# One fixed-order stream of 1 MB weight halves in the expert stage of a hybrid diffusion backbone

## The chip, the cores and the metric

One Trainium2 chip; the program runs on one of its cores. The metric is device microseconds of one execution. A page of the profile calls the engines PE (TensorE, with PEld for its weight loads), DVE (VectorE), ACT (ScalarE), POOL (GpSimd) and SP (the queue that issues most DMAs).

## What is computed

A trunk layer over 1024 tokens of width 1024: modulated RMSNorm, a token mixer, then an expert-choice MoE, and a last RMSNorm. Four fifths of the time goes to the MoE, in fp32:

```python
cap = EC_CAPACITY * n // N_EXPERTS          # 128 tokens for each of 16 experts
aff = softmax(h @ w_router)
g, idx = lax.top_k(swapaxes(aff, 1, 2), cap)
xg = h[bidx, idx]
hid = silu(xg @ w_gate) * (xg @ w_up)       # (128, 1024) @ (1024, 2816), twice
y = (hid @ w_down) * g[..., None]           # (128, 2816) @ (2816, 1024)
out = zeros_like(h).at[bidx, idx].add(y)
```

## The kernel before

After a prologue (the mixer, the router, and the token lists of experts 0 and 1), `moe` walks over 16 experts `e` and six column blocks `j` of each: five of 512 columns, one of 256. `gate_up(e, j)` multiplies the gathered tokens with a block of w_gate and of w_up, `down` of the block before multiplies its hidden block with rows of w_down into `y`.

A product in fp32 is made of three products of rounded parts (`mm3`, L607): ScalarE rounds a weight tile (`hi`, L226), VectorE subtracts (`lo`, L227), and TensorE multiplies x_hi by hi, x_hi by lo and x_lo by hi, in this order (L610). `xgh`/`xgl` are the parts of the tokens, `hh`/`hl` those of the hidden block. The weights are the moving operand.

Weights are loaded as 2 MB units into five raw slots `raw` (`load_unit`, L1535, DMA at L1541) and split in halves of 2048 columns into four `hi`/`lo` pairs (`hl_tile`, L1524), used in rotation: three pairs lie in the left pool `ma`, one in the right pool `mo`, where `xgh`, `xgl`, `hh` and `hl` lie too. A half is 12 matmuls of 512 columns (24 of 256 in the last block). Pair n is written again once TensorE has read it: with four pairs, the split of half m+4 waits for TensorE's last matmul of half m.

Beside the weights there are small steps:
- after each `gate_up`: `hid` (Silu on ScalarE at L1565, product on VectorE at L1566), four transposes `ht` on TensorE (L1570), `hh`, `hl`.
- once per expert `prep` (L1441): VectorE makes a one-hot tile `oh` (L1434), TensorE counts with it (`px`, L1437), VectorE sums to `idx` (L1439), GpSimd gathers the tokens `xg` (L1450), TensorE makes the gate values (`pg`, L1463). `prep_t` transposes the tokens (`xt`, L1483).
- at the end of an expert VectorE scales `y` into `ys` (L1595) and GpSimd adds it to the result in memory (L1596).
- during experts 0 and 1, 15 rounds of `topk_iter` find the thresholds of experts 2 to 15: `cand` (L1379) and `ge` (L1381) on VectorE, eight small matmuls `tc` on TensorE (L1385), then `g3`, `s3`, `inc`, `T` on VectorE (L1386 to L1389). `topk_end` makes the lists.

The order on each engine is set by the Tile scheduler, except for pinned instructions; `extra` (L1687) says in which block the small steps are recorded, not where they land.

Of the kernel before, what the change touches and what calls it, by code (L numbers as in the profile page):

```python
# [161 lines left out]
class Kern:  # L162
    HP, HT, LATE = 50, 300, -100

# [1210 lines left out]
    def topk_iter(self, i):  # L1375
        nc = self.nc
        V, G, T = nc.vector, nc.gpsimd, self.T
        cand, ge, g3, s3, inc = self.tk
        V.tensor_tensor(cand, self.pats[:, None, 3 * i:3 * i + 3].to_broadcast([128, E, 3]),  # L1379
                        T[:, :, None].to_broadcast([128, E, 3]), op=ALU.bitwise_or)  # L1380
        V.tensor_tensor(ge, self.lg[:, :, :, None].to_broadcast([128, 8, E, 3]),  # L1381
                        cand.bitcast(F32)[:, None].to_broadcast([128, 8, E, 3]), op=ALU.is_ge)
        pc = self.pt(f"tc{i}")[:, 0:3 * E]
        for b in range(8):
            nc.tensor.matmul(pc, self.ones2, ge[:, b].rearrange("p e q -> p (e q)"), start=b == 0, stop=b == 7)  # L1385
        V.tensor_scalar(g3.rearrange("p e q -> p (e q)"), pc, CAP - 0.5, None, op0=ALU.is_ge)  # L1386
        V.tensor_reduce(s3, g3, axis=mybir.AxisListType.X, op=ALU.add)
        V.tensor_scalar(inc, s3, float(1 << (28 - 2 * i)), None, op0=ALU.mult)
        V.tensor_tensor(T, T, inc, op=ALU.bitwise_or)  # L1389

    def topk_end(self):
# [21 lines left out]
        nb = need[:, None].to_broadcast([128, 8, E])  # L1413
        sel, sl = S("sel", [8, E]), S("sl", [8, E])
# [13 lines left out]
    NRAW, NHL = 5, 4  # L1428
    DL, DS, FROM = 2048, 1024, 95

    def pick(self, e, oh, p, idx, V):
        nc = self.nc
        slot = self.slot[:, e] if e < NR else self.slT[:, :, e]
        V.tensor_tensor(oh, self.iota[:, None, :].to_broadcast([128, 8, 128]),  # L1434
                        slot[:, :, None].to_broadcast([128, 8, 128]), op=ALU.is_equal)
        for b in range(8):
            nc.tensor.matmul(p[:, 0:2], oh[:, b], self.tokb[:, b], start=b == 0, stop=b == 7)  # L1437
        with nc.allow_low_precision(reason="whole numbers below 2**24"):
            V.tensor_reduce(idx, p[:, 0:2], axis=mybir.AxisListType.X, op=ALU.add)  # L1439

    def prep(self, e):  # L1441
        nc = self.nc
        if e == 0:
            idx = self.idx0
        else:
            self.oh = self.mo.tile([128, 8, 128], BF16, tag="oh", name=f"oh{e}", bufs=1)
            idx = self.mo.tile([128, 1], I32, tag="idx", name=f"idx{e}", bufs=3)
            self.pick(e, self.oh, self.pt(f"px{e}"), idx, nc.vector)
        xg = self.mo.tile([128, D], F32, tag="xg", name=f"xg{e}", bufs=1)
        nc.gpsimd.indirect_dma_start(out=xg, out_offset=None, in_=self.hxd,  # L1450
                                     in_offset=bass.IndirectOffsetOnAxis(ap=idx[:, :1], axis=0))
# [22 lines left out]
    def prep_t(self, e, pin=False):  # L1474
# [3 lines left out]
        lo = self.mo.tile([128, KD, 128], F32R, tag="xgl", name=f"xgl{e}", bufs=2)  # L1478
        for g in range(2):
# [4 lines left out]
            self.split(p.rearrange("p (k c) -> p k c", c=128), hi[:, 4 * g:4 * g + 4], lo[:, 4 * g:4 * g + 4], pin=pin)  # L1484
        self.xe[e] = (hi, lo, idx)

    def moe_open(self):
        self.ma = self.ctx.enter_context(self.tc.tile_pool(name="ma", bufs=1, side="left", reuse_waits="tile"))
        self.nu = self.nr = self.nh = 0
# [3 lines left out]
        self.first = [[self.hl_tile(f"0_{h}") for h in range(2)]]  # L1493

        a = self.a
        self.ahead = []
        for i, src in enumerate((a["wg"][0, 0], a["wu"][0, 0], a["wg"][0, 1], a["wu"][0, 1], a["wd"][0, 0])):
            raw = self.raw_tile(f"raw{i}")
            self.ahead.append(raw)
            if i < 4:  # L1500
                self.nc.sync.dma_start(raw, src)
        self.raw0, self.raw4 = self.ahead[0], self.ahead[4]
        self.ahead.pop(0)
        self.nu, self.n0 = 1, 0

    def hold(self, h):
        s = slice(2048 * h, 2048 * h + 2048)
        self.pin(self.nc.gpsimd.memset(self.raw4[:, 2048 * h:2048 * h + 1], 0.0))
        self.pin(self.nc.sync.dma_start(self.raw4[:, s], self.a["wd"][0, 0][:, s]))

    def unit0(self, A, G):
        c = 1024 * (self.n0 % 2)
        hi, lo = self.first[0][self.n0 // 2]
        src = self.raw0[:, 1024 * self.n0:1024 * self.n0 + 1024]
# [4 lines left out]
    def raw_tile(self, name):  # L1519
        t = self.ma.tile([128, 4096], F32, tag=f"raw{self.nr % self.NRAW}", name=name, bufs=1)  # L1520
# [9 lines left out]
    def unit_tiles(self, w):  # L1530
        out = [self.hl_tile(f"{self.nu}_{h}") for h in range(w // 2048)]
        self.nu += 1
        return out, self.ahead.pop(0) if self.ahead else None

    def load_unit(self, src, w=4096, fine=False):  # L1535
        out, raw = self.unit_tiles(w)
        if raw is None:
            raw = self.raw_tile(f"raw{self.nu}")
            n = self.DL if fine else w
            for c in range(0, w, n):  # L1540
                self.nc.sync.dma_start(raw[:, c:c + n], src[:, c:c + n])  # L1541
        n = self.DS if fine else 2048
        for h, (hi, lo) in enumerate(out):
            for c in range(0, 2048, n):
                self.split(raw[:, 2048 * h + c:2048 * h + c + n], hi[:, c:c + n], lo[:, c:c + n])
        return out

    def gate_up(self, e, j):
        nc, a = self.nc, self.a
        xh, xl = self.xe[e][:2]  # L1550
        p = self.pm.tile([128, 2, 512], F32, tag="gu", name=f"gu{e}{j}", bufs=2)
        w = 512 if j < 5 else 256
        if j < 5:
            us = self.first if e + j == 0 else []
            us = us + [self.load_unit(a[n][e, j]) for n in ("wg", "wu")[len(us):]]
        else:
            us = [[u] for u in self.load_unit(a["wt"][e], fine=6 * e + j >= self.FROM)]
        for g in range(2):
            nk = 8 // len(us[g])
            for k in range(KD):  # L1560
                hi, lo = us[g][k // nk]
                s = slice(w * (k % nk), w * (k % nk) + w)
                self.mm3(p[:, g, 0:w], xh[:, k], xl[:, k], hi[:, s], lo[:, s], k == 0, k == KD - 1)
        hid = self.mo.tile([128, 512], F32, tag="hid", name=f"hid{e}{j}", bufs=2)
        nc.scalar.activation(hid[:, 0:w], p[:, 0, 0:w], AF.Silu)  # L1565
        nc.vector.tensor_tensor(hid[:, 0:w], hid[:, 0:w], p[:, 1, 0:w], op=ALU.mult)  # L1566
        nb = w // 128
        q = self.pt(f"ht{e}{j}")
        for b in range(nb):
            nc.tensor.transpose(q[:, 128 * b:128 * b + 128], hid[:, 128 * b:128 * b + 128], self.ident)  # L1570
# [3 lines left out]
        return hh, hl, nb  # L1574

    def down(self, e, j, h):
        nc, a = self.nc, self.a
        hh, hl, nb = h
        if j == 0:
            self.y = self.pm.tile([128, D], F32, tag="y", name=f"y{e}", bufs=1)  # L1580
        fine = 6 * e + j >= self.FROM - 1
        u = self.load_unit(a["wd"][e, j], fine=fine) if j < 5 else self.load_unit(a["wdt"][e], 2048, fine=fine)
        if j == 5 and e == E - 1:
            self.last_loads()
        for b in range(nb):
# [185 lines left out]
```

## Time and profile before

| | |
|---|---|
| median of 3 runs | 2070.2 us (2068.81 to 2071.71) |
| the profiled execution | 2068.58 us, its span 2066.8 us |
| PE, PEld, DVE, ACT, POOL busy, of the span | 94%, 75%, 84%, 65%, 10% |
| mean granted TensorE clock | 0.977 |
| expert stage | from about 434 us to the end |
| weights and the rest moved | 651 MB, 315 GB/s over the span |

The span is cut in stages; what counts in a stage is the wait that ends last there, on TensorE. A matmul's recorded time (some 0.39 us) overlaps the next one's: what it costs is the distance from its start to the next start. Idle time of another engine costs nothing by itself.

### The profile page before, as it was taken

How to read it: one execution, taken by the hardware profiler on the slowest of the kernel's cores; microseconds unless marked ns; L12 is line 12 of the kernel's file. 1: busy time of each engine (PE TensorE's matmuls, PEld its weight loads, DVE VectorE, ACT ScalarE, POOL GpSimd, SP SyncE). 2: the span in 40 equal slices, each digit the busy share in tenths (PEclk: the TensorE clock that was granted, in tenths of full speed). 3: DMA queues.
4: the chain of work that ended last, by engine and by line, in shares of the span. 5: the costliest groups of instructions: out<-in, count | busy, mean ns of one | idle time of the engine just before them, and what ended most of it. 6: DMA issues, size and time to landing. Idle time of an engine off the chain costs nothing.

```text
span 2066.8 us, 23677 instructions
## 1 busy us (share of the span) xinstructions
PE 1942.7 (94%) x9434; PEld 1557.4 (75%) x9434; DVE 1741.0 (84%) x1641; ACT 1336.2 (65%) x1104; POOL 203.7 (10%) x141
## 2 busy tenths in 40 slices
PE   7989989969999999999999999999999999999994
PEld 2777778757877878787878787878787777878774
DVE  7888887799997888888888888888888788888876
ACT  6558633356775666666666676766766667666665
POOL 2311101220011000001010101010101010000011
PEclk9999999979999999999999999999999999999997
DMA  8444553679897989899898989898989898989894
GB/s 317 127 134 157 183 181 129 253 275 362 323 372 291 376 319 389 339 372 350 347 375 346 378 343 382 335 381 341 378 340 376 348 375 340 385 327 385 339 363 175
DMA packets 77517, 651.26 MB, mean 315 GB/s; under 512 B 8695, under 2 KB 16424, under 8 KB 42206
## 3 DMA queue, kind: packets, MB, share of 16 engines
q1 hardware_dynamic: 64286, 602.54, 74.6%
q0 software_dynamic: 10816, 38.82, 6.4%
q10 hardware_dynamic: 2304, 8.39, 1.0%
q8 instruction: 74, 1.21, 0.2%
q14 instruction: 37, 0.30, 0.0%
HBM read 622.98 MB, written 26.74 MB: 314 GB/s over the span
## 4 chain that ended last, share of the span: by engine, by line
PE 73%; DVE 12%; issue 5%; DMA 5%; ACT 3%; POOL 1%; SPq 0%; POOLq 0%; DVEq 0%; ACTq 0%
PE gu L610 44%; PE y L610 21%; DVE lo L227 5%; PE mx L610 3%; DMA mraw<-in_wmod_dram 3%; ACT hi L226 2%; PE ht L1570 2%; DMA wm<-in_wmod_dram 1%; DVE macc L838 1%; DVE ys L1595 1%; DMA trr<-in_trig_dram 1%; PE pq L610 1%; DVE g L715 1%; DMA accx<-xr 1%; DVE xgl L227 0%
## 5 line engine op out<-in xcount | busy, mean ns | idle before, releaser
L227 DVE TENSOR_TENSOR lo<-raw,hi 128x2048 fp32r<-128x2048 f32 (+1 forms) x531 | 1183.0, 2269 | 121.3 <-ACT hi L226 119.1
L226 ACT ACTIVATE hi<-raw 128x2048 fp32r<-128x2048 f32 (+1 forms) x531 | 982.8, 1894 | 92.7 <-PE gu L610 76.4
L610 PE MATMUL gu<-lo,xgh 128*128 128x512 f32 (+1 forms) x1536 | 586.1, 382 | 34.0 <-DVE lo L227 34.0
L610 PE MATMUL gu<-hi,xgh 128*128 128x512 f32 (+1 forms) x1536 | 581.0, 378 | 1.8 <-ACT xgh L226 1.6
L610 PE MATMUL gu<-hi,xgl 128*128 128x512 f32 (+1 forms) x1536 | 581.0, 378 | 1.7 <-DVE xgl L227 1.7
L610 PEld LDWEIGHTS gu<-lo,xgh 128*128 128x128 f32 x1536 | 289.9, 189 | 104.1 <-DVE lo L227 48.3
L610 PEld LDWEIGHTS gu<-hi,xgh 128*128 128x128 f32 x1536 | 290.2, 189 | 60.0 <-ACT xgh L226 2.1
L610 PEld LDWEIGHTS gu<-hi,xgl 128*128 128x128 f32 x1536 | 289.9, 189 | 57.6 <-DVE xgl L227 2.9
L610 PE MATMUL y<-hi,hl 128*128 128x512 f32 x704 | 283.2, 402 | 0.0
L610 PE MATMUL y<-lo,hh 128*128 128x512 f32 x704 | 281.5, 400 | 0.0
L610 PE MATMUL y<-hi,hh 128*128 128x512 f32 x704 | 278.1, 395 | 0.0
L1565 ACT ACTIVATE hid<-gu 128x512 f32<-128x512 f32 x96 | 54.0, 563 | 308.9 <-PE gu L610 308.9
L1596 POOL DMA_INDIRECT accx<-ys,idx x15 | 50.7, 3379 | 1147.4 <-DVE ys L1595 1071.8
L610 PEld LDWEIGHTS y<-lo,hh 128*128 128x128 f32 x704 | 132.5, 188 | 29.4
L610 PEld LDWEIGHTS y<-hi,hh 128*128 128x128 f32 x704 | 132.8, 189 | 28.2
L610 PEld LDWEIGHTS y<-hi,hl 128*128 128x128 f32 x704 | 132.8, 189 | 27.1
L1566 DVE TENSOR_TENSOR hid<-hid,gu 128x512 f32<-128x512 f32 x96 | 61.5, 640 | 67.9 <-ACT hid L1565 67.9
L226 ACT ACTIVATE hh<-ht 128x512 fp32r<-128x512 f32 x96 | 53.9, 561 | 94.4 <-PE ht L1570 94.4
L227 DVE TENSOR_TENSOR hl<-ht,hh 128x512 fp32r<-128x512 f32 x96 | 61.4, 640 | 4.5 <-ACT hh L226 4.5
L1450 POOL DMA_INDIRECT xg<-hxd,idx x16 | 42.3, 2643 | 213.1 <-DVE idx L1439 164.2
L838 DVE SCALAR_TENSOR_TENSOR macc<-mraw,cond,macc 128x512 f32<-128x512 f32 x56 | 41.8, 748 | 17.9 <-DMA mraw<-in_wmod_dram 17.0
L1570 PE MATMUL ht<-k_ident,hid 128*128 128x128 f32 x352 | 54.6, 274 | 1.7 <-DVE hid L1566 1.7
(425 smaller groups left out, 1866.3 us busy)
## 6 DMA issues: line engine op xcount, KB each, us to landing
raw<-in_wg_dram SPq DMA_DIRECT2D x80, 2048.0 KB, 9.5
raw<-in_wu_dram SPq DMA_DIRECT2D x80, 2048.0 KB, 10.6
raw<-in_wd_dram SPq DMA_DIRECT2D x78, 2048.0 KB, 9.8
raw<-in_wt_dram SPq DMA_DIRECT2D x15, 2048.0 KB, 9.9
mraw<-in_wmod_dram POOLq DMA_DIRECT2D x32, 512.0 KB, 4.6
raw<-in_wdt_dram SPq DMA_DIRECT2D x16, 1024.0 KB, 8.0
wm<-in_wmod_dram SPq DMA_DIRECT2D x16, 512.0 KB, 10.0
wr<-in_win_dram SPq DMA_DIRECT2D x24, 256.0 KB, 3.7
```

The lines of the kernel that those rows point to most:

```text
L226: i = self.nc.scalar.activation(hi, src, AF.Copy)
L227: j = (eng or self.nc.vector).tensor_tensor(lo, src, hi, op=ALU.subtract)
L610: i = nc.tensor.matmul(out, l, r, start=st, stop=sp)
L715: V.tensor_tensor_scan(g[:, s], a[:, s], r[:, s], 0.0, op0=ALU.mult, op1=ALU.add)
L838: nc.vector.scalar_tensor_tensor(acc, w[:, i], c, acc, op0=ALU.mult, op1=ALU.add)
L1450: nc.gpsimd.indirect_dma_start(out=xg, out_offset=None, in_=self.hxd, in_offset=bass.IndirectOffsetOnAxis(ap=idx[:, :1], axis=0))
L1565: nc.scalar.activation(hid[:, 0:w], p[:, 0, 0:w], AF.Silu)
L1566: nc.vector.tensor_tensor(hid[:, 0:w], hid[:, 0:w], p[:, 1, 0:w], op=ALU.mult)
L1570: nc.tensor.transpose(q[:, 128 * b:128 * b + 128], hid[:, 128 * b:128 * b + 128], self.ident)
L1595: nc.vector.scalar_tensor_tensor(ys, self.y, gate, self.g2b, op0=ALU.mult, op1=ALU.mult)
L1596: nc.gpsimd.indirect_dma_start(out=self.accx, out_offset=bass.IndirectOffsetOnAxis(ap=idx[:, :1], axis=0), in_=ys, in_offset=None, compute ...
```

## The change

The expert stage is written as one list of 1 MB halves (`make_stream`, 528 in all). For each half m, in this order, TensorE's 12 matmuls, the Silu and product if a block ends there, the split of half m+4, the load of half m+10, and then the small steps that a table (`plan`) hangs on m. TensorE, ScalarE and VectorE keep exactly this order (`manual_schedule`); SP and GpSimd do not. The raw slots become ten of 1 MB. A pad of 160 bytes at the bottom of `ma` moves its tiles: in the built program the three pairs of `ma` start at 288 modulo 512 before and at 448 after, the pair in `mo`, `xgh` and `xgl` at 448 in both; `hh` and `hl` start at 448 before and at 256 after. Finer pieces for the last loads (`FROM`, `DL`, `DS`) are gone.

```diff
@@ moe_open
+        self.ma.tile([128, self.PAD], F32, name="pad")
+        self.make_stream()
...
@@ make_stream
+            for j in range(6):
+                gu(e, j)
+                if prev is not None:
+                    dn(*prev)
+                prev = e, j
...
+    def load(self, m):
+        M = len(self.S)
+        if m < M:
+            self.raws[m] = self.raw_tile(f"raw{m}")
+            self.nc.sync.dma_start(self.raws[m], self.S[m][5])
...
+    def cut(self, m, pin=False):
+        if m >= len(self.S):
+            return
+        self.hls[m] = self.hl_tile(m)
+        self.split(self.raws.pop(m), *self.hls[m], pin=pin)
...
+    def plan(self):
...
+        s = self.at
+        at(1, self.g2_load)
+        at(3, self.gates)
+        at(3, self.topk_start)
+        for i in range(15):
+            at(5 + 3 * i, self.topk_a, i)
+            at(6 + 3 * i, self.topk_p, i)
+            at(7 + 3 * i, self.topk_b, i)
+        steps(50, self.topk_end())
...
+                at(m, self.hid_t, e, j)
+            if e + 1 < E:
+                steps(s[e, 4 if e == 1 else 1], self.prep(e + 1))
+                steps(s[e, 5 if e == 1 else 4], self.prep_t(e + 1), 1 if e == 1 else 2)
+                at(self.end[e + 1, 0] + 1, self.scatter, e)
...
@@ moe
+            ET = mybir.EngineType
+            st.enter_context(tc.manual_schedule(engines={ET.PE, ET.Activation, ET.DVE}))
...
+            for m in range(M):
+                self.half(m)
+                if m in self.end.values():
+                    self.act(*self.S[m][1:3])
+                self.cut(m + 4)
+                self.load(m + 10)
+                for f in post.pop(m, ()):
+                    f()
             self.last()
```

`topk_a` is `cand` and `ge`, `topk_p` the eight matmuls `tc`, `topk_b` the four small operations behind them. `steps` hangs the parts of `prep` (`oh`; `px`; `idx`, gather and `pg`; the gate) on one half after the other.

VectorE in a round of the threshold search (round 5), before; the number behind a name counts tiles, and `lo14_0` is the first half of unit 14:

```order
L227 TENSOR_TENSOR lo13_0_4291<-raw14_4294,hi13_0_4290 128x2048
L1381 TENSOR_TENSOR ge_3855<-lg_60,cand_3854 128x384
L227 TENSOR_TENSOR lo13_1_4293<-raw14_4294,hi13_1_4292 128x2048
L1386 TENSOR_SCALAR g3_3856<-tc5_4196 128x48
L1387 TENSOR_REDUCE s3_3857<-g3_3856 128x16
L1388 TENSOR_SCALAR inc_3858<-s3_3857 128x16
L1389 TENSOR_TENSOR T_3852<-T_3852,inc_3858 128x16
L227 TENSOR_TENSOR lo14_0_4372<-raw15_4375,hi14_0_4371 128x2048
```

In the change, VectorE in round 1, from the split of half 12 to that of half 15:

```order
L228 TENSOR_TENSOR lo12_3925<-raw12_3746,hi12_3924 128x2048
L1379 TENSOR_TENSOR cand_3780<-k_pats_2065,T_3778 128x48
L1381 TENSOR_TENSOR ge_3781<-lg_60,cand_3780 128x384
L228 TENSOR_TENSOR hl01_3938<-ht01_3932,hh01_3937 128x512
L228 TENSOR_TENSOR lo13_3954<-raw13_3767,hi13_3953 128x2048
L228 TENSOR_TENSOR lo14_3982<-raw14_3802,hi14_3981 128x2048
L1393 TENSOR_SCALAR g3_3782<-tc1_3959 128x48
L1394 TENSOR_REDUCE s3_3783<-g3_3782 128x16
L1395 TENSOR_SCALAR inc_3784<-s3_3783 128x16
L1396 TENSOR_TENSOR T_3778<-T_3778,inc_3784 128x16
L228 TENSOR_TENSOR lo15_4004<-raw15_3832,hi15_4003 128x2048
```

And TensorE in the same round, the end of half 9 and the first of the eight `tc`:

```order
L611 MATMUL y0_3911<-hi9_3828,hh00_3809 128x512
L611 MATMUL y0_3911<-lo9_3829,hh00_3809 128x512
L611 MATMUL y0_3911<-hi9_3828,hl00_3810 128x512
L1388 LDWEIGHTS ones2_3776
L1388 MATMUL tc1_3959<-ge_3781,ones2_3776 128x48
```

The candidates of a round now stand right behind the split of half m+4, and the matmuls that need them stand one half after m; before, both stood where the scheduler put them.

VectorE at the one-hot tile of expert 6, before (expert 4 is running: unit 73 belongs to it, and `px6` comes in expert 5):

```order
L1439 TENSOR_REDUCE idx5_6958<-px5_6959 128x1
L227 TENSOR_TENSOR lo73_1_6987<-raw74_6988,hi73_1_6986 128x2048
L1464 TENSOR_REDUCE gate5_6972<-pg5_6973 128x1
L1434 TENSOR_TENSOR oh6_7665<-k_iota_2063,slT_4946 128x1024
L227 TENSOR_TENSOR lo74_0_6995<-raw75_6998,hi74_0_6994 128x2048
```

In the change, VectorE around the same tile, in expert 5:

```order
L228 TENSOR_TENSOR lo172_7739<-raw172_7623,hi172_7738 128x2048
L1636 SCALAR_TENSOR_TENSOR ys4_7744<-y4_7118,gate4_6346,g2b_3687 128x1024
L228 TENSOR_TENSOR hl50_7753<-ht50_7747,hh50_7752 128x512
L228 TENSOR_TENSOR lo173_7770<-raw173_7648,hi173_7769 128x2048
L1447 TENSOR_TENSOR oh6_7775<-k_iota_2063,slT_5131 128x1024
L228 TENSOR_TENSOR lo174_7791<-raw174_7667,hi174_7790 128x2048
```

And TensorE there, the end of half 170 and the first of the eight `px`:

```order
L611 MATMUL gu51_7756<-hi170_7699,xgh5_7425 128x512
L611 MATMUL gu51_7756<-lo170_7700,xgh5_7425 128x512
L611 MATMUL gu51_7756<-hi170_7699,xgl5_7426 128x512
L1452 LDWEIGHTS oh6_7775
L1452 MATMUL px6_7796<-tokb_2551,oh6_7775 128x2
```

The one-hot tile was made an expert ahead of its use; now it is made behind the split of half 173 and used behind half 170.

## Rows read from the trace of the kernel before

**Rows 1.** Stage table: length; PE, PEld, DVE, ACT, POOL busy; granted clock; DMA share; GB/s.

```profile
700.00:1900.00 1200.00, 1170.34 (x5621) 948.69 (x5620) 1015.61 (x614) 816.00 (x566) 73.83 (x24) 1.00 0.92 358
```

**Rows 2.** Waits, 700 to 1900 us: us in total, times, longest; SP's own last.

```profile
PE gu L610 <- DVE lo L227: 29.7, 36, 1.4
ACT hi L226 <- PE gu L610: 27.9, 25, 1.6
SPq L1541 <- DVE lo L227: 1059.9, 193, 10.9
```

**Rows 3.** Chain that ended last: the same block's start, ten experts apart (start, us).

```profile
841.52 11.19 PE gu L610 x48
...
1836.14 11.19 PE gu L610 x48
```

**Rows 4.** Timeline of PE, 1010 to 1021 us: first matmuls of four halves in a row.

```profile
1010.20 0.39 PE L610 MATMUL gu<-hi,xgh 128*128 128x512 f32 x1
...
1012.96 0.40 PE L610 MATMUL gu<-hi,xgh 128*128 128x512 f32 x1
...
1021.38 0.40 PE L610 MATMUL y<-hi,hh 128*128 128x512 f32 x1
```

**Rows 5.** Timeline of PE in the prologue: first and fifteenth matmul of a run.

```profile
209.39 0.39 PE L610 MATMUL uf<-hTh,wl 128*128 128x512 f32 x1
...
212.57 0.39 PE L610 MATMUL uf<-hTl,wh 128*128 128x512 f32 x1
```

**Rows 6.** Timeline, 1052 to 1057 us: one split, from ACT over DVE to PE.

```profile
1052.07 1.91 ACT L226 ACTIVATE hi<-raw 128x2048 fp32r<-128x2048 f32 x1
...
1054.01 2.29 DVE L227 TENSOR_TENSOR lo<-raw,hi 128x2048 fp32r<-128x2048 f32 x1 [1.12 <-ACT hi L226]
...
1056.36 0.51 PE L610 MATMUL gu<-lo,xgh 128*128 128x512 f32 x1 [1.34 <-DVE lo L227]
```

**Rows 7.** Timeline of DVE: four splits in a row, and operations of the threshold search.

```profile
1040.06 8.90 DVE L227 TENSOR_TENSOR lo<-raw,hi 128x2048 fp32r<-128x2048 f32 x4 [0.56 <-ACT hi L226]
...
499.96 0.20 DVE L1379 TENSOR_TENSOR cand<-k_pats,T 128x48 int32<-128x48 int32 x1
500.19 0.56 DVE L1381 TENSOR_TENSOR ge<-lg,cand 128x384 bf16<-128x384 f32 x1
...
514.01 0.20 DVE L1386 TENSOR_SCALAR g<-tc 128x48 f32<-128x48 f32 x1
...
514.92 2.29 DVE L227 TENSOR_TENSOR lo<-raw,hi 128x2048 fp32r<-128x2048 f32 x1
```

**Rows 8.** Groups of DVE, 700 to 1900 us: count | busy us, mean ns | idle before.

```profile
L227 DVE TENSOR_TENSOR hl<-ht,hh 128x512 fp32r<-128x512 f32 x60 | 41.0, 684 | 0.0
L1595 DVE SCALAR_TENSOR_TENSOR ys<-y,gate,g2b 128x1024 f32<-128x1024 f32 x12 | 15.3, 1275 | 0.0
L1434 DVE TENSOR_TENSOR oh<-k_iota,slT 128x1024 bf16<-128x1024 f32 x11 | 13.4, 1215 | 0.0
```

**Rows 9.** Timeline of PE: first matmuls of halves 5 and 50 (experts 0, 1).

```profile
450.94 0.39 PE L610 MATMUL gu<-hi,xgh 128*128 128x512 f32 x1
...
589.70 0.39 PE L610 MATMUL gu<-hi,xgh 128*128 128x512 f32 x1
```

**Rows 10.** Timeline of PE with idle times; stage table behind the first of them.

```profile
621.20 0.35 PE L1437 MATMUL px<-tokb,oh 128*128 128x2 bf16 x8 [2.14 <-DVE oh L1434]
...
621.83:625.24 3.41, 3.41 (x11) 2.71 (x11) 3.41 (x4) 0.60 (x1) 3.00 (x1) 0.50 0.17 43
...
1972.54 0.50 PE L610 MATMUL gu<-lo,xgh 128*128 128x512 f32 x1 [1.83 <-DVE lo L227]
...
1975.34 0.63 PE L610 MATMUL gu<-hi,xgh 128*128 128x512 f32 x1
1975.76 0.63 PE L610 MATMUL gu<-lo,xgh 128*128 128x512 f32 x1
```

**Rows 11.** DMA issues: line, KB each, median us from issue to landing.

```profile
xg<-hxd,idx POOLq DMA_INDIRECT x16, 12.4
```

More of the change, by code (lines that the diff above doesn't have):

```diff
@@ L1492, in moe_open @@
         self.nr = 0
[L1493 to L1504, printed above, removed]
+        self.raws, self.hls = {}, {}
+        for m in range(2):
+            self.hls[m] = self.hl_tile(m)
+        for m in range(8):
+            self.load(m)
+        for m in range(8, 10):
+            self.raws[m] = self.raw_tile(f"raw{m}")
+        self.n0 = 0
     def hold(self, h):
-        s = slice(2048 * h, 2048 * h + 2048)
-        self.pin(self.nc.gpsimd.memset(self.raw4[:, 2048 * h:2048 * h + 1], 0.0))
-        self.pin(self.nc.sync.dma_start(self.raw4[:, s], self.a["wd"][0, 0][:, s]))
+        raw = self.raws[8 + h]
+        self.pin(self.nc.gpsimd.memset(raw[:, 0:1], 0.0))
+        self.pin(self.nc.sync.dma_start(raw, self.S[8 + h][5]))
     def unit0(self, A, G):
         c = 1024 * (self.n0 % 2)
-        hi, lo = self.first[0][self.n0 // 2]
-        src = self.raw0[:, 1024 * self.n0:1024 * self.n0 + 1024]
+        hi, lo = self.hls[self.n0 // 2]
+        src = self.raws[self.n0 // 2][:, c:c + 1024]
         A.activation(hi[:, c:c + 1024], src, AF.Copy)
@@ L1519, in raw_tile @@
     def raw_tile(self, name):
-        t = self.ma.tile([128, 4096], F32, tag=f"raw{self.nr % self.NRAW}", name=name, bufs=1)
+        t = self.ma.tile([128, 2048], F32, tag=f"raw{self.nr % self.NRAW}", name=name, bufs=1)
         self.nr += 1
@@ L1528, in hl_tile @@
         return [pool.tile([128, 2048], F32R, tag=f"{t}{i}", name=f"{t}{name}", bufs=1) for t in ("hi", "lo")]
[L1530 to L1555, printed above, removed]
-        else:
[L1557 to L1564, printed above, removed]
+    def load(self, m):
+        M = len(self.S)
+        if m < M:
+            self.raws[m] = self.raw_tile(f"raw{m}")
+            self.nc.sync.dma_start(self.raws[m], self.S[m][5])
+        elif m < M + 4:
+            t = 2 * (m - M)
+            src = self.accx.rearrange("(t p) c -> p t c", p=128)
+            self.fin.append(self.raw_tile(f"fin{t}"))
+            self.nc.sync.dma_start(self.fin[-1].rearrange("p (t c) -> p t c", t=2), src[:, t:t + 2])
@@ new lines, in cut, with half @@
+    def cut(self, m, pin=False):
+        if m >= len(self.S):
+            return
+        self.hls[m] = self.hl_tile(m)
+        self.split(self.raws.pop(m), *self.hls[m], pin=pin)
+    def half(self, m):
+        _, e, j, g, h, _ = self.S[m]
+        hi, lo = self.hls.pop(m)
+        if self.S[m][0] == "g":
+            xh, xl = self.xe[e][:2]
+            if g + h == 0:
+                self.gu[e, j] = self.pm.tile([128, 2, 512], F32, tag="gu", name=f"gu{e}{j}", bufs=2)
+            p = self.gu[e, j]
+            w = 512 if j < 5 else 256
+            nk = 2048 // w
+            for i in range(nk):
+                k, s = nk * h + i, slice(w * i, w * i + w)
+                self.mm3(p[:, g, 0:w], xh[:, k], xl[:, k], hi[:, s], lo[:, s], k == 0, k == KD - 1)
+        else:
+            if j + h == 0:
+                self.y = self.pm.tile([128, D], F32, tag="y", name=f"y{e}", bufs=1)
+            hh, hl = self.hid[e, j]
+            for i in range(2):
+                b = 2 * h + i
+                for n in range(2):
+                    s = slice(1024 * i + 512 * n, 1024 * i + 512 * n + 512)
+                    self.mm3(self.y[:, 512 * n:512 * n + 512], hh[:, 128 * b:128 * b + 128],
+                             hl[:, 128 * b:128 * b + 128], hi[:, s], lo[:, s], j == 0 and b == 0, j == 5 and i == 1)
@@ L1627, in last @@
         ys = self.mo.tile([128, D], F32, tag="ys", name="ysL", bufs=2)
-        part = lambda t: self.fin[t // 4][:, D * (t % 4):D * (t % 4) + D] if t < NT else ys
+        part = lambda t: self.fin[t // 2][:, D * (t % 2):D * (t % 2) + D] if t < NT else ys
         def y(t):
@@ L1722, in moe @@
             self.onesm = self.mo.tile([128, 128], F32, name="onesm")
-            prev = None
-            for e in range(E):
-                for j in range(6):
-                    h = self.gate_up(e, j)
-                    if prev is not None:
-                        self.down(*prev)
-                    prev = (e, j, h)
-                    with tc.issue_after(last.ins):
-                        self.extra(e, j)
-                    if j == (5 if e == 1 else 4) and e + 1 < E:
-                        self.prep_t(e + 1)
-                    if e == E - 1 and j == 1:
-                        self.last_prep()
-            self.down(*prev)
+            post = self.plan()
+            M = len(self.S)
+            for m in range(M):
[6 more added lines that the diff above has]
+                    f()
             self.last()
```

191 lines of the change are left out of this document (102 added, 89 removed).

## The prediction, made before the change was run

> **What bounds the kernel now.** I read the stage table first [rows 1]: from 700 to 1900 us PE is busy 1170 of 1200 us, at full granted clock, DVE 1016, ACT 816, and the DMA engines 0.92. So PE sets the pace, DVE (0.85) has a little room, and DMA must be looked at. The waits do that [rows 2]: the DMA queue itself waits 1060 of the 1200 us for a `lo` of DVE, that is for a raw slot to come free. The transfers are throttled by the consumer, not the other way round. PE in turn waits for `lo` 29.7 us in 36 waits, none over 1.4 us. The chain confirms it [rows 3]: the same block begins 994.67 us later ten experts on, so an expert costs 99.47 us, of which PE waits 29.7/12 = 2.5 us. All else is matmuls, and what one costs is read from starts [rows 4]: a half of 12 takes 2.76 us where moving and stationary tiles lie at the same address modulo 512 (every fourth half, the pair in `mo`), and the next three take 8.42 us, 2.81 us each: 230 and 234 ns per matmul. In the prologue, with both at 288, fifteen matmuls begin 227 ns apart ((212.57 - 209.39)/14) [rows 5].
>
> The second thing to know is how long a split takes from the moment its pair comes free: `hi` 1.91 us, hand-off 0.03, `lo` 2.29, hand-off 0.06 [rows 6]; four `lo` in a row take 8.90 us, 2.23 each [rows 7]. The pair comes free when PE's last matmul of the half four earlier ends, 0.4 us after its start [rows 4]. The execution that these rows come from took 2068.58 us (span 2066.8); the sum is made against that. The median of the three runs is 0.08% higher. A measurement of this kernel tells about 0.2%, 4 us, from no change.
>
> **The change part by part.**
>
> *Waits for `lo` at the blocks' seams.* In the fixed order the split of half m+4 stands behind half m, and DVE has three halves (8.4 us) for it, with 0.85 of its time taken. I take these waits as gone: 2.5 us x 14 experts = 35 us, and in the last expert one of 1.83 us with its low clock, in all **-38 us**. The other end is 0.
>
> *Addresses.* In `gate_up` all pairs come to lie at 448 like `xgh`. At the least that lifts three of four halves to the fourth: 20 halves x 0.75 x 0.05 us = 0.75 us an expert; at the most all 240 matmuls go to the 227 ns of the prologue and `y`'s 132 with them: 240 x 5.9 + 132 x 5.9 = 2.2 us (from their mean, 233). `hh` and `hl` move to 256, away from 448, so `y` may get nothing. I take the middle, 1.5 us an expert, x 15 = **-22 us**.
>
> *The rounds of the threshold search.* Here the order bites. `cand` and `ge` stand behind `lo` of half m+4, and the eight `tc` behind half m+1. From the start of half m's last matmul: 0.4 to its end, 0.05 hand-off (estimate), 1.91 `hi`, 0.03, 2.23 `lo`, `cand` 0.2 and `ge` 0.56 [rows 7], 0.06 hand-off: 5.4 us. PE is there after 12 matmuls and one more step, 3.0 us. It waits **2.4 us**, in every one of 15 rounds. Followed through one round, the next splits queue on DVE behind this one, and `g` to `T` take 0.91 us (514.01 to 514.92 [rows 7]) in front of a `lo`: I get 11.3 to 11.9 us for the three halves of a round. Before, 45 halves took 138.75 us [rows 9], 9.25 us for three, since the scheduler put `ge` far ahead of `tc`. 15 x 2.35 = **+35 us**. Bounds: 0, if `cand` and `ge` overtook (the printed order excludes it), and 15 x 3 = 45.
>
> *`px`.* The one-hot tile was made an expert early; now it stands behind `ys`, `hl` and two `lo`. From the last start of the half that ends an expert: `hi` done at 2.4, `lo` at 4.6, `ys` (1.28) 5.9, `hl` (0.68) 6.6, next `lo` 8.8, `oh` (1.22) 10.0 us [rows 8]. PE gets to `px` after four transposes and two halves, 6.0 to 6.4 us. It waits 3.6 to 4.0 us; 14 experts x 3.7 = **+52 us**, and 2 us for expert 1, where no `ys` stands ahead. The work itself is the same on either side; only its place is new.
>
> *The clock.* Where PE idled 2.14 us before `px` (at 621.20), the granted clock of the 3.41 us that follow is 0.50; after 1.83 us idle at 1972.54 matmuls start 0.42 us apart, the lower of the two levels (1.2 GHz instead of 2.4) [rows 10]. The waits of up to 1.4 us in rows 2 left the clock at 1.00 [rows 1]. A drop costs about 1.4 us (3.4 us at half rate, less what isn't matmul). The 29 waits above are 2.4 and 3.7 us; I count 0.85 of them: 29 x 0.85 x 1.4 = **+35 us**. Bounds: 0, and twice that.
>
> *The rest.* Twice as many DMA issues of half the size: bytes are the same, a load has ten halves less four (17 us) to land, and SP does little but wait [rows 2]. I take 0. Silu now stands ahead of the split of m+4 at each block's end, so that one comes later by one Silu, hidden by the three halves of lead. The gather of expert 2's tokens (12.4 us to land [rows 11]) meets PE at about the end of the first expert's stream as it did before: 0, plus or minus 5 (an estimate). The finer pieces of the last loads are gone: the last load now lands some 15 us (six halves) before its use, 0.
>
> Sum: -38 - 22 + 35 + 54 + 35 = +64, and 2068.6 + 64 = **2132 us**.
>
> A rule that speaks against the address part: the Trainium skill, "TensorE: Matmul & The Clock Gate", section "Step-by-step: what each phase is for", has two independent read ports of the array, one for the moving and one for the stationary operand, so that where these lie should not matter. By it the -22 would be 0 and the sum 2154. The trace doesn't agree, by a little: 2.76 against 2.81 us for the half with equal addresses [rows 4].
>
> **The rivals.**
>
> *The waits come but the clock holds.* Then the +35 falls away: 2097 us. For it: waits to 1.4 us left the clock alone, and 2.4 us is close to the 1.83 and 2.14 that did not; against it, these two both did. Chance 0.25.
>
> *Equal addresses free the array altogether (the other side).* At the lower clock a matmul takes 0.42 to 0.43 us [rows 10], so half of it, 213 ns, is what the columns alone need; today's 233 holds 20 ns of something else. If that is the reading of two operands that meet, and equal addresses remove it, 372 matmuls get some 15 ns beyond the 1.5 us taken: 5.8 us x 15 = -87 us, 2045 us. It decides for faster from about 12 ns beyond (64 us/(15 x 372)), a spacing near 217 ns. Against it: matmuls at equal addresses are there already, 227 and 230 ns apart [rows 4, 5], and `y` does not get them. Chance 0.12.
>
> The Trainium skill, the same page, section "Back-to-back issue gap", gives N/2.4 + 2.5 ns for a single warm gap, 216 ns for 512 columns; no run here shows it so far.
>
> *The addresses give nothing, or a drop lasts longer.* With no rate gain 2154; with drops of twice the length 2132 + 35 = 2167; with both 2189. For it: `hh` and `hl` are moved off `y`'s address, so the change does not do all that is said of it. Chance 0.15.
>
> **How the numbers follow.** My case (waits with drops, a part of the rate) has 0.48, 2105 to 2155; held clock 0.25, 2085 to 2110; the freed array 0.12, 2025 to 2070; the worse case 0.15, 2150 to 2190. The likeliest gives 2132. The range 2075 to 2165 leaves out the freed array and the upper half of the worse case, about 0.2. Slower by over 0.2%: all but the freed array and 0.04 for cases near 2070, 0.84; faster 0.12.
>
> **What would show it.** In experts 0 and 1: PE idle 2 to 3 us ahead of `tc`, released by `ge` of DVE, 15 times; three halves about 11.5 us apart instead of 9.25; that stretch some 50 us longer with its drops. Once an expert from 2 on: PE idle 3 to 4 us ahead of `px`, released by `oh`. The granted clock 0.50 behind both; in 700 to 1900 us a mean of 0.98 to 0.99 instead of 1.00. `gate_up`'s waits for `lo` near zero. A half of `gate_up` 2.72 to 2.76 us throughout, `y`'s 2.75 to 2.81. An expert of 100.4 us (99.5 - 2.5 - 1.5 + 3.7 + 1.2). I am wrong if `tc` and `px` find their operands ready, if PE's waits move to `lo`, or if matmuls run below 225 ns.

## The result, and the profile after the change

The changed kernel takes 2149.46 us (median of 4 runs, 2146.95 to 2152.06), the kernel before 2069.99 us beside it: a ratio of 1.0383, 95% interval 1.0365 to 1.0401, 79 us slower. The forecast was 2132 us, 64 us slower, in a range of 2075 to 2165. The profiled execution took 2149.83 us (span 2148.0), 81.2 us more than the span of before.

Where the 81 us lie, from the starts of each expert's first matmul: 2 us before expert 0, 43.9 in expert 0, 27.1 in expert 1, 0.1 in expert 2, 15.2 in the twelve experts 3 to 14, and 7.2 us less from expert 15 on. So nearly nine tenths were lost in two experts of 16.

The stage table of the changed kernel, for the first expert and a half and for the steady stretch (columns: length; PE, PEld, DVE, ACT and POOL busy; granted clock; DMA share; GB/s):

```profile
434.00:640.00 206.00, 162.51 (x759) 128.46 (x760) 141.33 (x167) 102.12 (x70) 6.01 (x8) 0.88 0.72 252
700.00:1900.00 1200.00, 1157.29 (x5554) 954.29 (x5553) 1021.13 (x610) 829.19 (x562) 30.91 (x24) 0.97 0.96 355
```

In the second, against [rows 1], the clock is 0.97 instead of 1.00 and PE idles 43 us instead of 30, though its matmuls have become faster. What PE waits for from 434 us on (the waits; us in total, times, longest):

```profile
PE px L1452 <- DVE oh L1447: 57.1, 15, 6.3
PE tc L1388 <- DVE ge L1381: 33.0, 14, 3.1
...
PE pg L1471 <- DVE idx L1455: 4.0, 1, 4.0
PE tcf L1409 <- DVE m L1405: 2.4, 1, 2.4
PE ht L1627 <- DVE g L1393: 1.8, 1, 1.8
```

(`tcf` are the two counting matmuls at the start of `topk_end`.) Not one wait for `lo` is left of those in [rows 2]; the two forecast ones have come in their place. A round of the threshold search, in the timeline of DVE (start us, us):

```profile
492.19 0.20 DVE L1393 TENSOR_SCALAR g<-tc 128x48 f32<-128x48 f32 x1
...
492.97 2.29 DVE L228 TENSOR_TENSOR lo<-raw,hi 128x2048 fp32r<-128x2048 f32 x1
495.17 0.20 DVE L1379 TENSOR_TENSOR cand<-k_pats,T 128x48 int32<-128x48 int32 x1
495.41 0.56 DVE L1381 TENSOR_TENSOR ge<-lg,cand 128x384 bf16<-128x384 f32 x1
```

and of PE, idle time and its releaser in brackets:

```profile
490.55 0.39 PE L611 MATMUL gu<-hi,xgh 128*128 128x512 f32 x1
...
496.03 0.37 PE L1388 MATMUL tc<-ge,ones 128*128 128x48 bf16 x8 [2.60 <-DVE ge L1381]
...
498.06 0.63 PE L611 MATMUL gu<-hi,xgh 128*128 128x512 f32 x1
499.33 0.63 PE L611 MATMUL gu<-hi,xgh 128*128 128x512 f32 x1
```

Half m ends with a matmul that starts 0.23 us before 490.55; `tc` comes 5.7 us after it, where 5.4 was worked out: the four small operations from 492.19 on stand in front of the `lo`, as forecast. Rounds behind whose wait the clock held come 11.2 us apart, close to the 11.3 to 11.9 worked out; most of the others take 13.2 to 13.7 us. Behind the wait three matmuls take 1.27 us instead of 0.68: the lower clock. `px` of expert 6, in the timeline of DVE:

```profile
1030.35 4.61 DVE L228 TENSOR_TENSOR lo<-raw,hi 128x2048 fp32r<-128x2048 f32 x2 [0.32 <-ACT hi L227]
1034.88 1.28 DVE L1636 SCALAR_TENSOR_TENSOR ys<-y,gate,g2b 128x1024 f32<-128x1024 f32 x1
1036.08 0.68 DVE L228 TENSOR_TENSOR hl<-ht,hh 128x512 fp32r<-128x512 f32 x1
1036.67 2.28 DVE L228 TENSOR_TENSOR lo<-raw,hi 128x2048 fp32r<-128x2048 f32 x1
1038.87 1.22 DVE L1447 TENSOR_TENSOR oh<-k_iota,slT 128x1024 bf16<-128x1024 f32 x1
```

on PE:

```profile
1040.15 0.37 PE L1452 MATMUL px<-tokb,oh 128*128 128x2 bf16 x8 [3.57 <-DVE oh L1447]
```

and in the stage table for the stretch from 1040.02 us and for the one in the next expert:

```profile
1040.02:1043.43 3.41, 3.28 (x15) 2.70 (x16) 2.27 (x2) 0.00 (x0) 0.00 (x0) 0.50 1.00 263
1139.01:1145.84 6.83, 5.43 (x20) 4.02 (x20) 3.54 (x3) 0.00 (x0) 0.00 (x0) 0.50 1.01 296
```

This is the chain of the forecast, `lo`, `ys`, `hl`, `lo`, `oh`, and the wait is the 3.6 us worked out. The drop takes 3.41 us in one expert and 6.83 in the next, by turns, and an expert takes 100.2 and 101.2 us (99.5 before, 100.4 forecast).

Three waits were not in the sum (timeline of PE, experts 0 and 1):

```profile
460.44 0.37 PE L1452 MATMUL px<-tokb,oh 128*128 128x2 bf16 x8 [4.47 <-DVE oh L1447]
470.54 0.35 PE L1471 MATMUL pg<-aux,oh 128*128 128x3 bf16 x8 [4.05 <-DVE idx L1455]
686.71 0.37 PE L1452 MATMUL px<-tokb,oh 128*128 128x2 bf16 x8 [6.34 <-DVE oh L1447]
```

Last, the spacing of matmuls in a steady stretch: first matmuls of two `gate_up` halves in a row, and the first and tenth of a `y` half.

```profile
716.32 0.39 PE L611 MATMUL gu<-hi,xgh 128*128 128x512 f32 x1
...
719.04 0.39 PE L611 MATMUL gu<-hi,xgh 128*128 128x512 f32 x1
...
724.48 0.40 PE L611 MATMUL y<-hi,hh 128*128 128x512 f32 x1
...
726.58 0.39 PE L611 MATMUL y<-hi,hh 128*128 128x512 f32 x1
```

A `gate_up` half takes 2.72 us (227 ns a matmul) against 2.76 and 2.81 in [rows 4]; `y` has 2.10/9 = 233 ns, as before.

### The profile page after: what moved, and what is told of

Read it like the earlier page. It is cut to its first block, busy times and chain, and to the rows that moved or that the text cites. A ratio compares the mean times of both kernels' runs of the same rounds, so it can differ in the third digit from the quotient of the medians.

```text
span 2148.0 us, 24524 instructions
## 1 busy us (share of the span) xinstructions
PE 1959.5 (91%) x9434; PEld 1590.1 (74%) x9434; DVE 1760.1 (82%) x1636; ACT 1361.1 (63%) x1099; POOL 151.4 (7%) x141
## 4 chain that ended last, share of the span: by engine, by line
PE 72%; DVE 13%; issue 6%; DMA 5%; ACT 4%; POOL 1%; SPq 0%; POOLq 0%; ACTq 0%; DVEq 0%
PE gu L611 41%; PE y L611 21%; DVE lo L228 5%; PE mx L611 4%; ACT hi L227 3%; DMA mraw<-in_wmod_dram 3%; PE ht L1627 1%; DVE oh L1447 1%; DVE macc L839 1%; PE xt L1499 1%; DVE ys L1636 1%; PE hp L1181 1%; DMA trr<-in_trig_dram 1%; PE pq L611 1%; DMA wr<-in_win_dram 0%
## 5 line engine op out<-in xcount | busy, mean ns | idle before, releaser
L228 DVE TENSOR_TENSOR lo<-raw,hi 128x2048 fp32r<-128x2048 f32 x526 | 1207.7, 2297 | 258.6 <-ACT hi L227 256.9
L227 ACT ACTIVATE hi<-raw 128x2048 fp32r<-128x2048 f32 x526 | 1008.6, 1918 | 441.5 <-PE gu L611 302.0
L611 PE MATMUL gu<-hi,xgh 128*128 128x512 f32 (+1 forms) x1536 | 599.9, 391 | 0.0
L611 PE MATMUL gu<-hi,xgl 128*128 128x512 f32 (+1 forms) x1536 | 590.1, 384 | 0.0
L611 PEld LDWEIGHTS gu<-hi,xgl 128*128 128x128 f32 x1536 | 300.8, 196 | 56.0 <-DVE xgl L228 0.2
L611 PEld LDWEIGHTS gu<-lo,xgh 128*128 128x128 f32 x1536 | 301.9, 197 | 52.7
L611 PEld LDWEIGHTS gu<-hi,xgh 128*128 128x128 f32 x1536 | 301.3, 196 | 52.0 <-ACT xgh L227 0.2
L611 PE MATMUL y<-hi,hh 128*128 128x512 f32 x704 | 286.6, 407 | 0.0
L1637 POOL DMA_INDIRECT accx<-ys,idx x15 | 23.8, 1589 | 1284.4 <-DVE ys L1636 1284.4
L1452 PE MATMUL px<-tokb,oh 128*128 128x2 bf16 x128 | 6.0, 168 | 61.6 <-DVE oh L1447 57.1
L1627 PEld LDWEIGHTS ht<-k_ident,hid 128*128 128x128 f32 x352 | 44.3, 141 | 17.0 <-DVE g L1393 2.2
```

The costliest lines, as they stand in the source:

```text
L227: i = self.nc.scalar.activation(hi, src, AF.Copy)
L228: j = (eng or self.nc.vector).tensor_tensor(lo, src, hi, op=ALU.subtract)
L611: i = nc.tensor.matmul(out, l, r, start=st, stop=sp)
L1627: self.nc.tensor.transpose(q[:, c:c + 128], hid[:, c:c + 128], self.ident)
L1637: self.nc.gpsimd.indirect_dma_start(out=self.accx, out_offset=bass.IndirectOffsetOnAxis(ap=idx[:, :1], axis=0), in_=ys, in_offset=None, co ...
```

## The experiments

The theory: the order itself is not slow, but a few steps stand on TensorE before VectorE can have their operand ready; each such wait costs itself and a stretch at the low clock. Rivals: VectorE's fixed order is too slow as a whole, so a wait removed comes back elsewhere; the clock falls for another reason; the addresses give nothing, or everything. The kernel before took 2067 to 2070 us beside each; ratios are to it.

### `tc` one half later

```diff
-            at(6 + 3 * i, self.topk_p, i)
+            at(7 + 3 * i, self.topk_p, i)
```

> The eight tc of each round stand one half later (7 + 3i instead of 6 + 3i), everything else stays. My theory (TensorE waits because the place of tc comes 2.4 us before ge is ready, and each such wait is followed by a stretch at the low clock): the 33 us of waits for ge go, and with them some 18 us of slow matmuls, 2149 - 51 = about 2098 us; the three halves of a round come down from about 13 to under 10 us. Rival A (VectorE's fixed order is itself too slow, so the wait moves to lo or to the next ge): above 2135 us, with the waits for ge or lo still 20 us or more. Rival B (the clock falls there whatever TensorE waits for): 2116 us, with as many stretches at 0.50 as before.

Measured: 2093.6 us, ratio 1.0121 (1.0102 to 1.0141), 56 us less than the change; 51 were expected. The waits and the stage table:

```profile
PE px L1452 <- DVE oh L1447: 57.1, 15, 6.3
...
PE tc L1388 <- DVE ge L1381: 0.9, 1, 0.9
```

```profile
434.00:640.00 206.00, 184.79 (x945) 147.55 (x946) 179.29 (x208) 126.10 (x86) 17.65 (x17) 0.94 0.89 321
```

The waits for `ge` are gone but for 0.9 us, the clock of the stretch went from 0.88 to 0.94, and no other wait of their size took their place. The 4.0 us wait for `pg` went too, which the forecast had not counted. Moving 15 groups of eight tiny matmuls by 2.7 us gave back 56 us.

### `cand` and `ge` ahead of the split

```diff
+                if m in self.early:
+                    self.topk_a(self.early[m])
                 self.cut(m + 4)
```

> The change with cand and ge ahead of the split of half m + 4 on VectorE instead of behind it; tc stays where the change has it, one half later. My theory (what TensorE waits for at tc is VectorE's queue, the split ahead of ge, and nothing of ge itself): the 33 us of waits go as they do with tc later, about 2098 us. Rival (the split that now stands behind cand and ge comes late instead, or the search's own chain of g to T and cand to tc is what takes the time): above 2120 us with waits for ge or lo of 15 us or more.

Measured: 2107.54 us, ratio 1.0187 (1.0170 to 1.0204). The waits:

```profile
PE tc L1388 <- DVE ge L1381: 6.4, 12, 1.0
PE pg L1471 <- DVE idx L1455: 4.2, 1, 4.2
```

It is the same wait, taken away from the other side: 42 us gone, from 33.0 us of waits to 6.4, with none over 1.0 us; none of these short ones was followed by the low clock. What remains of them is most of the 9 us by which it falls short of the forecast. So it was the split ahead of `ge` in VectorE's queue that TensorE waited for.

### The one-hot tile earlier, `px` later

```diff
-                steps(s[e, 4 if e == 1 else 1], self.prep(e + 1))
+                steps(s[e, 4 if e == 1 else 1] - (e > 1), self.prep(e + 1), 3 if e > 1 else 1)
```

> From expert 3's tokens on, the one-hot tile stands one half earlier, ahead of the lo it stood behind, and px two halves behind its old distance to it, so px comes one half later than in the change; idx and the gather follow later too. My theory: 13 waits of 3.6 us for oh go (46 us) and with them the stretches at the low clock behind them, some 18 us of slow matmuls: about 2085 us, an expert about 95.8 us instead of 100.7, the granted clock from 815 us on 1.00. Rival A (another wait of the same chain takes the place: pg, xt behind the gather, or lo): above 2120 us and a new wait of 2 us or more per expert. Rival B (the clock doesn't hang on these waits): about 2103 us with stretches at 0.50 still once per expert.

Measured: 2101.09 us, ratio 1.0161 (1.0141 to 1.0181), 48 us less than the change; 64 were expected. The stage table and the waits:

```profile
700.00:1900.00 1200.00, 1181.51 (x5784) 976.03 (x5783) 1059.21 (x634) 862.88 (x584) 32.45 (x26) 1.00 0.99 368
```

```profile
PE pg L1471 <- DVE hl L228: 20.0, 13, 1.5
```

The theory and its rival A both have a part, though rival A's 2 us an expert and 2120 us did not come. The waits for `oh` and the low clock are gone from the steady stretch, an expert takes 96.97 us. But `pg` now stands where the one of two PSUM tiles that it takes still holds the hidden block's transposes: 1.5 us, 13 times, is the missing 16 us and more. That it is this tile fits the releaser `hl`, and the run with the rest of the waits taken out, below, puts `pg` one half further back and has none of these waits. The 13 waits here were not followed by the low clock.

### TensorE kept at work during the waits

Matmuls whose result is overwritten are added ahead of `tc` and `px`; nothing is moved.

```diff
+        self.dummy(self.pc, 0 if i < 9 else 1, 9)
...
+        if e > 1:
+            self.dummy(p, e - 1, 14)
```

> The waits stay, but TensorE is kept at work in them: 9 matmuls of 512 columns ahead of each tc, 14 ahead of px from expert 2's tokens on, into the same PSUM tile, whose contents px and tc then overwrite. It adds 15 x 9 + 14 x 14 matmuls and takes none away. My theory (idle time makes the clock fall, and the fall costs some 38 us in all): the stretches at 0.50 behind tc and px go, the time from the last real matmul to tc or px is unchanged, 2149 - 35 = about 2115 us. Rival A (the clock falls for another reason, or its fall costs nothing because other engines set the pace): 2145 to 2155 us. Rival B (the added matmuls cost their full time, because the waits are not waits): 2149 + 331 x 0.23 = about 2225 us.

Measured: 2109.46 us, ratio 1.0207 (1.0183 to 1.0230): with 331 more matmuls, 40 us less than the change. The stage table:

```profile
700.00:1900.00 1200.00, 1195.34 (x5826) 988.21 (x5825) 1041.54 (x619) 847.03 (x572) 30.91 (x24) 1.00 0.97 362
```

The `px` of the same expert as above, with its 14 added matmuls (timeline of PE):

```profile
1012.48 0.39 PE L611 MATMUL gu<-hi,xgl 128*128 128x512 f32 x1
1012.71 3.33 PE L1388 MATMUL px<-xgl,xgh 128*128 128x512 f32 x14
1016.44 0.35 PE L1462 MATMUL px<-tokb,oh 128*128 128x2 bf16 x8 [0.40 <-DVE oh L1455]
```

From the last real matmul to `px` it is 3.96 us, as in the change (1036.19 to 1040.15). So the operand of `px` comes no earlier here, and an expert still came down from 100.7 to 98.8 us, with the clock at 1.00. That separates the wait from its echo: of the cost, some 40 us is the clock alone.

### The address of the weights

```diff
-        self.ma.tile([128, self.PAD], F32, name="pad")
```

> The change without its pad: three of the four pairs of weight parts lie at 288 modulo 512 again, the tokens' parts at 448. My theory (equal addresses bring gate_up's matmuls from 232.5 to 227.6 ns, all on the path): 240 x 4.9 ns x 16 experts = 19 us slower than the change, about 2168 us; gate_up's halves 2.80 us instead of 2.72 for three in four. Rival A (the faster matmuls came with the order, not the address): 2149 us and halves of 2.72 us. Rival B (the waits take up the difference, since VectorE sets when tc and px may start): 2150 to 2158 us, with slower matmuls and shorter waits.

Measured: 2166.23 us, ratio 1.0473 (1.0450 to 1.0497), 17 us slower than the change. First matmuls of two halves in a row (timeline of PE):

```profile
715.30 0.40 PE L611 MATMUL gu<-hi,xgh 128*128 128x512 f32 x1
...
718.11 0.39 PE L611 MATMUL gu<-hi,xgh 128*128 128x512 f32 x1
```

2.81 us again. The address, not the order, made `gate_up` faster.

### The address of the hidden block

`off` and `need`, two small tiles, are allocated ahead of `hh` and `hl`, so these start at 448.

```diff
+        self.offn = S("off", [2, 9, E]), S("need", [E])
...
-        off = S("off", [2, 9, E])
+        off, need = self.offn
```

> The change with hh and hl at 448 modulo 512, where the weight parts lie (256 in the change). My theory: y's matmuls come from 233.5 to 227.6 ns apart like gate_up's, 132 x 5.9 ns x 16 = 12 us, about 2137 us. Rival A (for y the address of the stationary operand doesn't count): 2149 us, 233 ns. Rival B (an even larger part of the 20 ns over the columns' own 213 goes): 372 x 10 ns x 16, under 2100 us.

Measured: 2138.85 us, ratio 1.0342 (1.0318 to 1.0366), 11 us less than the change. First and tenth matmul of the same `y` half as above (timeline of PE):

```profile
724.54 0.39 PE L611 MATMUL y<-hi,hh 128*128 128x512 f32 x1
...
726.58 0.39 PE L611 MATMUL y<-hi,hh 128*128 128x512 f32 x1
```

2.04/9 = 227 ns. `y` gains like `gate_up`, once its two operands are at one address; in the change they were not.

### The pad alone, in the kernel before

```diff
+        self.ma.tile([128, 40], F32, name="pad")
```

> The kernel before with the pad alone: all pairs, xgh, xgl, hh and hl at 448 modulo 512, nothing else moved. My theory (the address part is worth its matmuls): gate_up from 232.5 and y from 232.7 to about 227.5 ns, (240 x 5 + 132 x 5.2) x 16 = 30 us faster than before, about 2040 us. Rival A (TensorE then runs into lo more often, since the splits don't get faster): waits for lo grow from 2.5 us an expert to 4 us or more and the time is 2055 to 2070 us. Rival B (addresses do nothing without the fixed order): 2070 us, 233 ns.

Measured: 2043.39 us, ratio 0.9875 (0.9853 to 0.9898): one line makes the old kernel 25 us faster. The waits:

```profile
PE gu L610 <- DVE lo L227: 34.6, 40, 1.8
```

They stay at what they were, 34.0 us in the profile before; an expert takes 97.7 us instead of 99.5.

### All three parts together

> tc one half later, the one-hot tile earlier and px later as in the two runs before, and hh and hl at 448 modulo 512 like the weights (two small tiles of the threshold search are allocated earlier). My theory, the gains add up: 2149 - 51 - 64 - 12 (132 matmuls of y by 5.9 ns by 16 experts) = about 2022 us, an expert 95 us, y's matmuls 227 ns apart. Rival A (without the waits TensorE runs into lo or into the raw slots, as before the change): 2040 to 2070 us, with waits for lo of 2 us or more per expert. Rival B (y's addresses do nothing): about 2034 us, y's matmuls still 233 ns apart.

Measured: 2036.03 us, ratio 0.9851 (0.9831 to 0.9870): 14 us short of the sum. The waits:

```profile
PE pg L1471 <- DVE hl L228: 20.7, 13, 1.6
PE px L1452 <- DVE oh L1447: 10.7, 2, 6.5
```

No wait for `lo`, so it is not rival A, though 2036 us is close to its range; it is again `pg`, and the two `px` of experts 0 and 1, which this table didn't touch.

### The rest of the waits taken out

```diff
+                q = s[e, 1]
+                each(self.prep(e + 1), *((2, 4, 4, 6, 6), (54, 57, 57, 59, 59))[e] if e < 2 else (q - 1, q + 2, q + 2, q + 6, q + 6))
...
+            at(4 + 3 * i, self.topk_a, i)
+            at(6 + 3 * i, self.topk_p, i)
+            at(6 + 3 * i, self.topk_b, i)
+        each(self.topk_end(), 49, 51, 51, 52)
```

The numbers are the halves on which one-hot tile, `px`, gather, `pg` and gate hang. The two matmuls of `g2_row` move as well, from the last block of expert 0 to halves 16 and 17.

> The run with all three parts, with the rest of the waits taken out by the table: from the tokens of expert 3 on pg stands four halves behind px instead of three and apart from the gather, so the PSUM tile that it takes (there are two in turn) is free; in expert 0 the one-hot tile stands two halves earlier and px one, idx and pg no longer in one step; the threshold search starts one half earlier, tcf stands two halves behind m, px of expert 2 three halves behind its one-hot tile. My theory (only places that come too early for VectorE cost anything): 13 waits of 1.6 us for pg, px 4.2 and 6.5, tcf 2.2, tc 2.3 and some 7 us of slow matmuls go, 2036 - 43 = about 1994 us, an expert 94.8 us. Rival (the DMA engines, busy 0.99 of the stretch from 700 to 1900 us in that run, are the bound now): the waits move to hi for a raw slot's load, an expert stays at 96 us and more, 2020 to 2036 us.

Measured: 1997.68 us, ratio 0.9651 (0.9637 to 0.9665): 72 us faster than the kernel before and 152 faster than the change, with the change's own operations in other places. The stage table:

```profile
700.00:1900.00 1200.00, 1198.67 (x5906) 997.23 (x5906) 1080.87 (x646) 882.98 (x597) 32.41 (x25) 1.00 0.99 377
```

PE is busy 1198.67 of 1200 us and no wait of it is listed there. An expert takes 94.72 us. The DMA engines, busy 0.99, do not bound; their queue waited 921 of the 1200 us for a `lo` to free a slot:

```profile
SPq L1585 <- DVE lo L228: 920.8, 369, 4.7
```

### The fixed order by itself

The last kernel without the pad, so with the addresses of the kernel before.

> The same table of places as in the run with all waits taken out, without the pad: addresses as in the kernel before (three pairs at 288, one at 448, tokens and hidden block at 448 modulo 512). It is what the fixed order is worth by itself. My theory: matmuls 232.5 ns apart again, (240 x 5 + 132 x 4.5) x 16 = 29 us slower than with equal addresses, about 2023 us, and some 45 us faster than the kernel before, whose waits for lo (40) and clock drops it doesn't have. Rival (the order is worth nothing, the gain of the other run is all address): 2060 to 2075 us.

Measured: 2023.73 us, ratio 0.9780 (0.9765 to 0.9796). In the stage table PE is busy without a break:

```profile
700.00:1900.00 1200.00, 1200.00 (x5823) 982.19 (x5822) 1066.76 (x637) 868.88 (x589) 30.88 (x24) 1.00 0.99 371
```

So the fixed order, with this table of places and loads of 1 MB, is worth 46 us, and the addresses 26 on it and 25 on the old order.

### Raw slots of 2 MB

```diff
+        h = self.nr % 2
+        if h == 0:
+            self.pair = self.ma.tile([128, 4096], F32, tag=f"raw{self.nr % self.NRAW // 2}", name=name, bufs=1)
...
+        return self.pair[:, 2048 * h:2048 * h + 2048]
```

> The version with all waits taken out, with five raw slots of 2 MB, each loaded by two transfers of 1 MB, instead of ten of 1 MB; nothing else differs. A slot now comes free only when both of its halves are split, so half of the loads start one half (2.7 us) later. My theory (loads have some six halves to land, so when a slot comes free doesn't count): 1998 us within 4. Rival (with the DMA engines busy 0.99 of the time the loads are at their limit, and a later start reaches hi): 2005 us and more, with waits of hi for a load in most experts.

Measured: 2000.58 us, ratio 0.9666 (0.9653 to 0.9679), against 0.9651 (0.9637 to 0.9665) with ten slots: no difference that can be told. Ten slots of 1 MB instead of five of 2 MB were no part of the result that these runs can see. The transfers were 1 MB in both; what their size is worth by itself was not run.

The matmuls' distances from start to start at full clock (those up to 300 ns), as means over the steady stretch from about 820 us on, beside the addresses modulo 512:

| kernel | weights | tokens | hidden block | `gate_up`, ns | `y`, ns |
|---|---|---|---|---|---|
| before | 288 (3 of 4), 448 | 448 | 448 | 232.4 | 232.7 |
| the change | 448 | 448 | 256 | 227.6 | 233.5 |
| the change without pad | 288 (3 of 4), 448 | 448 | 256 | 232.6 | 233.4 |
| hidden block at 448 | 448 | 448 | 448 | 227.3 | 228.4 |
| pad alone | 448 | 448 | 448 | 227.0 | 228.4 |
| the fixed order by itself | 288 (3 of 4), 448 | 448 | 448 | 232.6 | 232.5 |

## Why the prediction was right, step by step

The sign, the mechanism and the range held; the time was 17 us longer than the forecast: against the sum, the clock came out 9 us dearer, the addresses gave 6 us less, the rest cost 6 us instead of nothing and the waits for `lo` gave 4 us less. By its steps:

- *Waits for `lo`* (-38): they went, all 34 us of them.
- *Addresses* (-22): `gate_up` gained 4.9 ns a matmul and `y` lost 0.8, so (240 x 4.9 - 132 x 0.8) x 15 = -16 us. For `gate_up` the prologue's 227 ns [rows 5] was the right row, not the 230 ns of the equal half in [rows 4]. That `y` would get nothing, since `hh` and `hl` had moved away from 448, was said and then half counted. That the middle of the two bounds came within 6 us is in part luck: `gate_up` got nearly all of its gain and `y` none.
- *The rounds* (+35): 33.0 us of waits. The two experiments from either side show the cause.
- *`px`* (+54): 57.1 us against 2.1 before [rows 10], so +55. The 3.6 us per expert was exact; expert 1's is 4.5 us, not 2, and expert 2's 6.3, not 3.7.
- *The clock* (+35): the step that was mis-sized. The matmuls in the stretches at 0.50 lose 50.5 us against their distance at full clock, summed one by one, and 6.3 us before: +44. The number was right, 27 stretches for 25 counted; but ten of them last 6.83 us and lose 2.4 to 2.9 us, not 1.4; the short ones lose about 1.5. So the mean clock from 700 to 1900 us is 0.97, where 0.98 to 0.99 was named. The row of a short drop [rows 10] was taken for all, though a long one stood in the same trace (stage table of before):

```profile
642.31:649.13 6.82, 6.23 (x15) 4.89 (x16) 1.14 (x2) 1.55 (x1) 0.00 (x0) 0.50 0.89 357
```

- *The rest* (0): `pg` of expert 1 (4.0), `tcf` (2.4) and `ht` (1.8 and 0.7) are 9 us against 5 us of like waits before, and expert 0 begins 2 us later, as it does, by 1 to 6 us, in the other runs of the fixed order with the same prologue. `pg` stands too early like the others, but not for its operand: it takes one of two PSUM tiles in turn, `tc` of the first round took the other, and its own is that of `px` until `idx` has read it. With `tc` one half later, behind `pg`, that wait is gone.

Together -34 - 16 + 33 + 55 + 44 + 4 + 2 = +88, against 81.2 in the spans; the parts come from different views, and 7 us of them are not told apart.

Of the rivals: the clock did fall, so 2097 us was out. That equal addresses free the array altogether is refuted: with all operands at 448, matmuls are 227 to 228 ns apart, not 217 or less. (Its gain was summed a little high: 372 matmuls by 15 ns by 15 experts are 84 us, not 87.) Of the third rival one half came true: drops of twice the length, for ten of the 27. That the addresses give nothing is refuted too: the runs with and without the pad differ by 17 us in the change and 25 us in the kernel before. The Trainium skill, "TensorE: Matmul & The Clock Gate", section "Step-by-step: what each phase is for", states two independent read ports, one for each operand. That the place of the operands therefore does not matter is not stated there; it was the prediction's conclusion, and the runs show that it does not hold here. The 216 ns that the Trainium skill, "TensorE: Matmul & The Clock Gate", section "Back-to-back issue gap", gives for a single warm gap was the spacing of these streams in no run here.

## What to carry to other kernels

When an order is written by hand, count for each small step on TensorE how far behind its producer's place it stands, in the producer's queue time (here 5.4 us), not in positions: here a step one unit of work (2.7 us) behind had to wait and two units behind it did not. A wait on the bounding engine as long as those of `tc` and `px` (1.9 us and more) is to be priced twice, once as itself and once as the slow stretch that mostly came with it. A change that bundles an order with an address layout should be measured in its parts: here 88 us of waits and 44 of their echo hid a good order and good addresses, worth 46 and 26 us.

## What the runs showed of the hardware that was not expected

- Matmuls of 512 columns with fp32 parts start 227 to 228 ns apart when moving and stationary tile lie at the same address modulo 512 (448 in five kernels here, 288 in the prologue), and 232 to 233 ns when they don't. It holds whatever the order, and was undone and redone by a pad of 160 bytes. Where only every fourth pair was equal, its half came to 230 ns [rows 4], not 227. Why, no run here shows; other pairs of addresses were not tried, and with 288, 448 and 256 a modulus of 128 or 256 would fit as well as 512.
- In the change the low clock came with each `px` wait of 3.6 us, lasting 3.41 and 6.83 us by turns, and with 11 of 13 waits of 1.9 to 3.1 us for `tc`. It is no fixed rule: in the change without its pad, 12 of 13 `px` waits of 3.4 to 3.5 us and 9 of 13 for `tc` drew it. Of 26 waits of 1.5 to 1.6 us (for `pg`, two kernels) two drew one, and of twelve of up to 1.0 us none. With TensorE busy on matmuls that nobody needs in these waits of `tc` and `px` (from expert 2's tokens on), none came with those of `tc` and one with those of `px`, and the kernel was 40 us faster for 331 more matmuls.
- DMA engines busy 0.99 of the time did not hold TensorE, busy 0.999 beside them.
